# A hybrid attention encoder layer in fp32 on one core: where the exponentials of the first query tiles are kept, and which engine casts and sums them

## The chip, the cores and the metric

The program runs on one core of a Trainium2 chip. The metric is device time in microseconds (us), the median of three runs. One execution was also profiled, instruction by instruction.

The core's engines work side by side, each through its own list of instructions in order: TensorE (PE: matmuls; PEld: its weight loads), VectorE (DVE), ScalarE (ACT), GpSimd (POOL), and SyncE (SP), which issues the DMAs. Matmuls write PSUM, which the kernel uses as eight banks of 128x512 fp32. VectorE and ScalarE read and write PSUM and SBUF; GpSimd's work here is all on SBUF tiles.

## The reference, cut to what matters

One encoder layer over 2048 tokens of width 1024. One input projection feeds two groups of attention heads; the change concerns group A, global attention with 8 query heads on 2 key/value heads of 64 columns.

```python
def global_attention(q, k, v):        # group A; B is windowed, |i - j| <= 128, with a sink logit
    ...
    def one_block(qi):
        s = jnp.einsum('bqkgd,bskd->bkgqs', qi, k).astype(jnp.float32) * scale
        p = jax.nn.softmax(s, axis=-1).astype(v.dtype)
        return jnp.einsum('bkgqs,bskd->bqkgd', p, v)
...
out_a = global_attention(qa, ka, va)
out_b = window_attention(qb, kb, vb, sink_b[l])
mixed = jnp.concatenate([rms_norm(out_a, group_norm_a[l]),
                         rms_norm(out_b, group_norm_b[l])], axis=-1) @ w_out[l]
x = x + rms_norm(mixed, norm_mix_post[l])
h = rms_norm(x, norm_ffn_pre[l])
f = (jax.nn.silu(h @ w_gate[l]) * (h @ w_up[l])) @ w_down[l]
x = x + rms_norm(f, norm_ffn_post[l])
```

## The kernel before

The kernel goes through four stages: input projection with group B's attention (from the start to about 486 us), group A's attention with the output projection (to about 1285 us), the FFN's gate and up products, and its down product. The inner matmuls take fp32r operands, and precision is kept by splitting a value in two: `hi`, the value cast to fp32r, and `lo`, the rest, value minus `hi`; products with `hi` and `lo` are added up in PSUM.

Group A is swept in units (t, g, kt): query tile t (16 tiles of 128 queries), key/value head g (2), key tile kt (16), so 32 units per tile. `attn` writes one unit as:

- two matmuls put the scores, 128 keys by 4 heads x 128 queries, into a PSUM bank (`sc`; the tiles are named `mm`, three banks, and `a`; in tile 0 `ow`, `o` and two `a` as well);
- ScalarE takes the exponential, as a rule in place in that bank; with t < `T_PF` and kt in `DVE_HI0` it goes to an SBUF tile `pfa` instead, of which there are `N_PF` = 2;
- `pha`, the cast to fp32r, by VectorE where kt is in `DVE_HI0` (t < `T_HI`) or `DVE_HI` (later tiles), else by ScalarE;
- `pla` = exponential - `pha`, by VectorE: the bank (or `pfa`) is free after it;
- the softmax's denominator needs the sum of all exponentials over the keys. For kt in `POOL_KT0` (t < `T_PK`) or `POOL_KT` (later) GpSimd adds `pha` to a running tile `acc` (of n such units n-1 adds); for the other kt TensorE does it, with one more matmul of `pha` by a ones matrix (`pha,z`);
- four units later (`AHEAD`), two matmuls of `pha` and `pla` with the values (`vt`).

Behind each (t, g) the sum `acc` is split (`aha`, `ala`) and added by two matmuls, and the denominator goes through DMAs to a reciprocal (`dena`, `cmpa`). The output projection of tile t-1 (`ow<-wo`) is interleaved with tile t from tile 2 on. Tile 0 and the start of tile 1 are interleaved with the tail of group B (its names: `pf`, `ph`, `pl`, `RB`, `R2B`, `VB`, `K1B`, `rb`, `oT`).

Every operation goes through a recorder (so all have line L515 in the profile), and a planner then lists them per engine: it simulates the engines with the cost formulas of `Plan.cost`, picks for each engine the first operation that could start, ranks anew, and keeps the best of four passes. Any edit of `attn` therefore moves other instructions too. `Plan.cost` prices a cast of an SBUF tile at 69 + 0.52 n ns, one of a PSUM bank at 69 + 1.042 n, and a subtraction at 69 + 1.042 n wherever its operands lie.

A second copy of the attention and all behind it, `general`, stands under a condition at the end and isn't executed with these inputs.

Of the kernel before, what the change touches and what calls it, by code (L numbers as in the profile page):

```python
# [10 lines left out]
F32 = mybir.dt.float32  # L11
F32R = mybir.dt.float32r
AF = mybir.ActivationFunctionType
# [5 lines left out]
P = 128  # L19
S = 2048  # L20
D = 1024
NT = S // P
# [17 lines left out]
NM = 5  # L40
LAG = AHEAD + LATE + RC + NM + 2
POOL_KT = tuple(k for k in range(NT) if k != 7)
POOL_KT0 = tuple(k for k in range(NT) if k not in (3, 7, 11))
DVE_HI = (2, 6, 10)
DVE_HI0 = (1, 3, 5, 7, 9, 11, 13)
PREP_NS = 500
P1W = 16000
XP_NS = 400
# [22 lines left out]
WD_L = 13  # L71
WD_R = 3
TAIL = 3
N_PF = 2
T_PF = 3
B_DVE = 13
B_DVE_U = (0, 2)
T_HI = 3
T_PK = 2
DEN_UP = 3000.0  # L80
HALF_UP = 8000.0
LAST_UP = 5000.0
# [5 lines left out]
def f32(ap):  # L88
    return ap.bitcast(F32)
# [428 lines left out]
class Layer:  # L518
# [743 lines left out]
    def attn(self):  # L1262
        nc = self.nc
        units = [(t, g, kt) for t in range(NT) for g in range(2) for kt in range(NT)]
        pend, acc, XY, out, later, norm = {}, {}, {}, {}, {}, {}
        for u in range(len(units) + AHEAD + LATE + 6):
            self.unit = u
            if u < len(units):
                t, g, kt = units[u]
                if g == 0 and kt == 8:  # L1270
                    self.qt.pop(t - 1, None)
                    self.load_q(t + 1)
                if t == g == 0 and kt == 0 and not self.shifted:
                    self.load_kv(NT // 2 - 1)
                if self.shifted and g == kt == 0:
                    self.load_shift(t)
                R1 = self.qt[t]
                sc = self.s_bank(t, g)
                k = self.k_part(self.kt[kt // 2], kt % 2)[:, g * P:(g + 1) * P]
                nc.tensor.matmul(sc, lhsT=k, rhs=R1[:, g, :], start=True, stop=False)  # L1280
                nc.tensor.matmul(sc, lhsT=k, rhs=self.qs[t, g], start=False, stop=not self.shifted)
                if self.shifted:
                    nc.tensor.matmul(sc, lhsT=self.ones_row, rhs=self.sh_row[t][:, g, :], start=False, stop=True)
                pf = sc
                if t < T_PF and kt in DVE_HI0 and not self.shifted:
                    pf = self.kv.tile([P, 512], F32, tag="pfa", bufs=N_PF, name="pfa")
                nc.scalar.activation(pf, sc, AF.Exp, scale=self.up_s if self.shifted else 1.0)
                sc = pf
                ph = self.kv.tile([P, 512], F32R, tag="pha", bufs=NPH, name="pha")
                pl = self.kv.tile([P, 512], F32R, tag="pla", bufs=NPL, name="pla")  # L1290
                if kt in (DVE_HI if t >= T_HI else DVE_HI0):
                    nc.vector.tensor_copy(ph, sc)
                else:
                    nc.scalar.activation(ph, sc, AF.Copy)
                nc.vector.tensor_tensor(pl, sc, f32(ph), op=ALU.subtract)
                if kt in (POOL_KT if t >= T_PK else POOL_KT0):
                    a = acc.get((t, g))
                    if a is None:
                        acc[t, g] = ph
                    elif a.dtype == F32R:  # L1300
                        acc[t, g] = self.kv.tile([P, 512], F32, tag="acc", name="acc")
                        nc.gpsimd.tensor_tensor(acc[t, g], f32(a), f32(ph), op=ALU.add)
                    else:
                        nc.gpsimd.tensor_tensor(a, a, f32(ph), op=ALU.add)
                pend[u] = ph, pl
                yield 432
            if 0 <= u - AHEAD < len(units):
                t, g, kt = units[u - AHEAD]
                ph, pl = pend.pop(u - AHEAD)
                f, l = kt == 0, kt == NT - 1  # L1310
                if f:
                    XY[t, g] = self.xy_banks(t, g)
                X, Y = XY[t, g]
                v = self.v_part(self.vt[kt // 4], kt % 4)[:, g * 192:(g + 1) * 192]
                nc.tensor.matmul(X, lhsT=v[:, 0:P], rhs=ph, start=f, stop=l)
                nc.tensor.matmul(Y, lhsT=v[:, HD:192], rhs=pl, start=f, stop=False)
                if kt not in (POOL_KT if t >= T_PK else POOL_KT0):
                    nc.tensor.matmul(Y, lhsT=self.z1, rhs=ph, start=False, stop=False)
                if l:
                    if g == 0:  # L1320
                        first = t == 0 and not self.shifted
                        pool = self.kv if first else self.op
                        out[t] = (pool.tile([P, 512], F32, tag="oa", bufs=1 if first else 2, name="oa"),
                                  pool.tile([P, 512], F32, tag="dena", bufs=1, name="dena"),
                                  self.sm.tile([16, HD], F32, tag="cmp", bufs=2, name="cmpa"))
                    oa = out[t][0]
                    nc.scalar.activation(oa[ROWS[g]], X[HD:P], AF.Copy)
                    nc.vector.tensor_tensor(oa[ROWS[g]], X[0:HD], oa[ROWS[g]], op=ALU.add)
                    later[u + LATE] = t, g
                yield 432  # L1330
            if u in later:
                t, g = later.pop(u)
                oa, den, cmp = out[t]
                X, Y = XY.pop((t, g))
                a = acc.pop((t, g))
                ah = self.kv.tile([P, 512], F32R, tag="aha", bufs=1, name="aha")
                al = self.kv.tile([P, 512], F32R, tag="ala", bufs=1, name="ala")
                nc.scalar.activation(ah, a, AF.Copy)
                nc.vector.tensor_tensor(al, a, f32(ah), op=ALU.subtract)
                nc.tensor.matmul(Y, lhsT=self.z1, rhs=ah, start=False, stop=False)  # L1340
                nc.tensor.matmul(Y, lhsT=self.z1, rhs=al, start=False, stop=True)
                if t < NT - 1:
                    self.den_row(den, Y, cmp, g)
                else:
                    self.urgent(HALF_UP)
                    nc.scalar.activation(den[ROWS[g]], Y[HD:P], AF.Copy)
                nc.vector.tensor_tensor(oa[ROWS[g]], Y[0:HD], oa[ROWS[g]], op=ALU.add)
                self.urgent(0.0)
                if g == 1:
                    norm[u + (RC if t < NT - 1 else 1)] = t, 0  # L1350
                yield 432
            if u in norm:
                t, j = norm.pop(u)
                oa, den, cmp = out[t]
                if t == NT - 1:
                    self.normalize(oa, den, j)
                    done = j == 3
                    norm[u + 1] = t, j + 1
                elif j == 0:
                    self.recip(cmp, self.RDA[t])  # L1360
                    self.spread(den, self.RDA[t])
                    done = False
                    norm[u + NM] = t, 1
                else:
                    nc.vector.tensor_tensor(oa, oa, den, op=ALU.mult)
                    done = True
                if done:
                    norm.pop(u + 1, None)
                    self.fin[t] = oa
# [444 lines left out]
```

## Time and profile before

| | |
|---|---|
| median of 3 runs | 2609.32 us (2606.59 to 2612.66) |
| the profiled execution | 2609.2 us; its span, first to last instruction, 2607.5 us |
| busy in the span | PE 2485.7 us, DVE 2008.2, POOL 1486.2, ACT 1411.9 |

The profile gives busy times by engine, the busy share in 40 slices of the span (65.2 us each), groups of like instructions, the waits, and the same for any stretch. "Busy" of PE counts the time in which some matmul is under way, at whatever clock; "PEclk" is the granted clock, with 1.00 for 2.4 GHz.

### The profile page before, as it was taken

The page shows a single profiled execution, that of the slowest core. Times are in us where ns is not written, and L with a number is a line of the kernel's source. Part 1 is how long each engine was busy: PE and PEld are TensorE (multiplying, and loading weights), DVE is VectorE, ACT ScalarE, POOL GpSimd, SP SyncE. Part 2 cuts the span into 40 slices and gives each one's busy share as a digit, 9 for nine tenths or more (in the row PEclk, how much of TensorE's full clock was granted, in tenths as well). Part 3 has the DMA queues.
Part 4 walks back from the last instruction along what each step waited for, and adds up shares of the span by engine and source line. Part 5 has one row for each costly group of instructions (what it writes and reads, how often), then busy time and mean ns, then how long its engine had stood idle before and what let it go on. Part 6 is the DMA issues. An engine that isn't in the chain of part 4 may idle for free.

```text
span 2607.5 us, 34089 instructions
## 1 busy us (share of the span) xinstructions
PE 2485.7 (95%) x10636; PEld 1957.9 (75%) x10636; DVE 2008.2 (77%) x3028; ACT 1411.9 (54%) x2622; POOL 1486.2 (57%) x1124
## 2 busy tenths in 40 slices
PE   8999999888999999999999999999999999999997
PEld 6666666555777778777778888778888887888886
DVE  7888887889889998988886767787566566556665
ACT  5666665666888888877543333343323324433443
POOL 3333333458989899999546566655465453422333
PEclk9999999999999999999999999999999999999999
DMA  5233332414222121333354455463332327654564
GB/s 163 100 124 124 123 98 81 142 41 171 68 69 99 56 94 65 114 110 106 106 172 143 146 178 161 155 217 130 108 107 89 113 86 228 191 177 149 182 197 155
DMA packets 187839, 334.88 MB, mean 128 GB/s; under 512 B 23808, under 2 KB 77440, under 8 KB 187136
## 3 DMA queue, kind: packets, MB, share of 16 engines
q1 hardware_dynamic: 187648, 332.61, 38.9%
q8 instruction: 86, 1.41, 0.2%
q14 instruction: 105, 0.86, 0.1%
HBM read 221.46 MB, written 106.56 MB: 126 GB/s over the span
## 4 chain that ended last, share of the span: by engine, by line
PE 57%; DVE 3%; POOL 2%; issue 2%; DMA 1%; ACT 0%; SPq 0%; DVEq 0%; POOLq 0%; ACTq 0%
PE gu L515 29%; PE gv L515 18%; PE ow L515 3%; PE mm L515 3%; PE o L515 3%; PE a L515 2%; POOL acc L515 1%; DVE pla L515 0%; DVE xl L515 0%; DVE wl L515 0%; DVE st L515 0%; POOL C L515 0%; DVE C L515 0%; DVE al L515 0%; DVE c L515 0%
## 5 line engine op out<-in xcount | busy, mean ns | idle before, releaser
L515 POOL TENSOR_TENSOR acc<-acc,pha 128x512 f32<-128x512 f32 x408 | 576.8, 1418 | 71.1 <-ACT pha L515 31.1
L515 POOL TENSOR_TENSOR s<-wraw 128x512 f32<-128x512 f32 x88 | 127.7, 1469 | 319.4 <-DMA wraw<-in_w_up_dram 167.9
L515 PE MATMUL gu<-xh,wl 128*128 128x512 f32 x776 | 279.6, 397 | 5.0 <-DVE wl L515 5.0
L515 PE MATMUL gu<-xh,wh 128*128 128x512 f32 x776 | 281.4, 397 | 0.6 <-ACT wh L515 0.6
L515 PE MATMUL mm<-R,kt 128*128 128x512 f32 x740 | 262.9, 403 | 18.9 <-DVE pla L515 16.5
L515 PE MATMUL gu<-xl,wh 128*128 128x512 f32 x776 | 279.8, 397 | 0.0
L515 PE MATMUL pp<-w_in,xh 128*128 128x512 f32 x720 | 239.8, 406 | 13.7 <-ACT w_in L515 9.2
L515 DVE TENSOR_TENSOR pla<-mm,pha 128x512 fp32r<-128x512 f32 x349 | 231.8, 679 | 22.6 <-ACT pha L515 15.6
L515 ACT ACTIVATE wh<-s 128x512 fp32r<-128x512 f32 x176 | 110.0, 629 | 254.1 <-PE gu L515 136.3
L515 DVE TENSOR_TENSOR al<-ar,ah 128x512 fp32r<-128x512 f32 x154 | 137.8, 900 | 134.7 <-ACT ah L515 115.4
L515 POOL TENSOR_TENSOR c<-c,c 128x512 f32<-128x512 f32 x132 | 200.2, 1531 | 63.9 <-DVE c L515 48.6
L515 ACT ACTIVATE mm<-mm 128x512 f32<-128x512 f32 x349 | 203.3, 590 | 44.6 <-PE mm L515 37.5
L515 ACT ACTIVATE ah<-ar 128x512 fp32r<-128x512 f32 x154 | 96.6, 629 | 206.1 <-PE gu L515 136.6
L515 DVE TENSOR_TENSOR c<-gu,c 128x512 f32<-128x512 f32 x174 | 117.5, 684 | 103.1 <-PE gu L515 98.0
L515 DVE TENSOR_TENSOR wl<-s,wh 128x512 fp32r<-128x512 f32 x176 | 172.6, 987 | 24.4 <-PE gu L515 18.4
L515 PEld LDWEIGHTS mm<-R,kt 128*128 128x128 f32 x740 | 138.1, 191 | 62.2 <-DVE pla L515 30.5
L515 ACT ACTIVATE wh<-wraw 128x512 fp32r<-128x512 f32 x132 | 83.1, 630 | 185.6 <-PE gu L515 92.5
L515 PE MATMUL ow<-wo,oh 128*128 128x512 f32 x488 | 176.6, 396 | 0.6 <-DVE ms L515 0.6
L515 PEld LDWEIGHTS gu<-xh,wl 128*128 128x128 f32 x776 | 146.1, 189 | 40.4 <-DVE wl L515 6.2
L515 PEld LDWEIGHTS gu<-xh,wh 128*128 128x128 f32 x776 | 146.3, 189 | 35.0 <-ACT wh L515 1.1
L515 PEld LDWEIGHTS gu<-xl,wh 128*128 128x128 f32 x776 | 146.6, 189 | 34.3
L515 PEld LDWEIGHTS pp<-w_in,xh 128*128 128x128 f32 x720 | 134.8, 191 | 47.3 <-ACT w_in L515 10.7
(268 smaller groups left out, 6720.9 us busy)
## 6 DMA issues: line engine op xcount, KB each, us to landing
AC<-c SPq DMA_DIRECT2D x154, 256.0 KB
ar<-AC SPq DMA_DIRECT2D x154, 256.0 KB
wdr<-in_w_down_dram SPq DMA_DIRECT2D x99, 256.0 KB
wraw<-in_w_gate_dram SPq DMA_DIRECT2D x20, 1024.0 KB
wraw<-in_w_up_dram SPq DMA_DIRECT2D x20, 1024.0 KB
st<-XB SPq DMA_DIRECT2D x40, 256.0 KB
QA<-RA SPq DMA_DIRECT2D x16, 512.0 KB
R<-QA SPq DMA_DIRECT2D x64, 128.0 KB
```

Source lines behind the costliest of these rows:

```text
L515: op.call(*[real(a) for a in op.args], **{k: real(v) for k, v in op.kw.items()})
```

## The change

In `attn` the exponentials of all units are now taken in place in PSUM; the two `pfa` tiles are gone (`N_PF`, `T_PF`). The tables for the first tiles change:

| per (t, g) of 16 units | before, t = 0 | t = 1 | t = 2 | after, t = 0 | t = 1 | t = 2 | both, t >= 3 |
|---|---|---|---|---|---|---|---|
| exponentials in `pfa` | 7 | 7 | 7 | 0 | 0 | 0 | 0 |
| casts on VectorE | 7 | 7 | 7 | 5 | 3 | 3 | 3 |
| units summed by GpSimd | 13 | 13 | 15 | 11 | 15 | 15 | 15 |
| ones matmuls on TensorE | 3 | 3 | 1 | 5 | 1 | 1 | 1 |

So from t = 1 on every tile is now treated as those from t = 3 on were before.

```diff
--- before.py
+++ after.py
@@ -40,9 +40,9 @@
 NM = 5
 LAG = AHEAD + LATE + RC + NM + 2
 POOL_KT = tuple(k for k in range(NT) if k != 7)
-POOL_KT0 = tuple(k for k in range(NT) if k not in (3, 7, 11))
+POOL_KT0 = tuple(k for k in range(NT) if k not in (2, 5, 8, 11, 14))
 DVE_HI = (2, 6, 10)
-DVE_HI0 = (1, 3, 5, 7, 9, 11, 13)
+DVE_HI0 = (1, 4, 7, 10, 13)
 PREP_NS = 500
 P1W = 16000
 XP_NS = 400
@@ -71,12 +71,10 @@
 WD_L = 13
 WD_R = 3
 TAIL = 3
-N_PF = 2
-T_PF = 3
 B_DVE = 13
 B_DVE_U = (0, 2)
-T_HI = 3
-T_PK = 2
+T_HI = 1
+T_PK = 1
 DEN_UP = 3000.0
 HALF_UP = 8000.0
 LAST_UP = 5000.0
@@ -1281,11 +1279,7 @@
                 nc.tensor.matmul(sc, lhsT=k, rhs=self.qs[t, g], start=False, stop=not self.shifted)
                 if self.shifted:
                     nc.tensor.matmul(sc, lhsT=self.ones_row, rhs=self.sh_row[t][:, g, :], start=False, stop=True)
-                pf = sc
-                if t < T_PF and kt in DVE_HI0 and not self.shifted:
-                    pf = self.kv.tile([P, 512], F32, tag="pfa", bufs=N_PF, name="pfa")
-                nc.scalar.activation(pf, sc, AF.Exp, scale=self.up_s if self.shifted else 1.0)
-                sc = pf
+                nc.scalar.activation(sc, sc, AF.Exp, scale=self.up_s if self.shifted else 1.0)
                 ph = self.kv.tile([P, 512], F32R, tag="pha", bufs=NPH, name="pha")
                 pl = self.kv.tile([P, 512], F32R, tag="pla", bufs=NPL, name="pla")
                 if kt in (DVE_HI if t >= T_HI else DVE_HI0):
```

The planner's lists show what this makes of the engines' order. First VectorE, in the second half of tile 1 (`oa` closes a head of tile 0 or 1, `ala` a sum). Before:

```order
L515 TENSOR_TENSOR pla<-pfa,pha 128x512
L515 TENSOR_TENSOR oa<-o_5956,oa 64x512
L515 TENSOR_TENSOR pla<-mm,pha 128x512
L515 CAST pha<-pfa 128x512 x2
L515 TENSOR_TENSOR pla<-pfa,pha 128x512
L515 TENSOR_TENSOR pla<-mm,pha 128x512
L515 TENSOR_TENSOR pla<-pfa,pha 128x512
L515 TENSOR_TENSOR ala<-acc,aha 128x512
L515 TENSOR_TENSOR pla<-mm,pha 128x512
L515 CAST pha<-pfa 128x512 x2
L515 TENSOR_TENSOR pla<-pfa,pha 128x512
```

and with the change:

```order
L513 TENSOR_TENSOR oa<-o_5962,oa 64x512
L513 TENSOR_TENSOR pla<-a_6140,pha 128x512
L513 TENSOR_TENSOR pla<-mm,pha 128x512 x2
L513 CAST pha<-mm 128x512
L513 TENSOR_TENSOR pla<-mm,pha 128x512
L513 TENSOR_TENSOR ala<-acc,aha 128x512
L513 TENSOR_TENSOR pla<-a_6190,pha 128x512
L513 TENSOR_TENSOR pla<-mm,pha 128x512 x2
L513 CAST pha<-mm 128x512
L513 TENSOR_TENSOR oa<-a_5953,oa 64x512
L513 TENSOR_TENSOR pla<-mm,pha 128x512
```

The casts and subtractions on `pfa` are gone; nearly all that is left between the closing operations is `pla` from a bank, with a cast from a bank here and there.

Next ScalarE, near the end of tile 2 (`sqo`: squares for the output projection's norm). Before:

```order
L515 ACTIVATE pha<-mm 128x512
L515 ACTIVATE pfa<-a_6607 128x512
L515 ACTIVATE sqo<-oa 128x512
L515 ACTIVATE pfa<-mm 128x512
L515 ACTIVATE pha<-mm 128x512
L515 ACTIVATE mm<-mm 128x512 x2
L515 ACTIVATE pfa<-a_6660 128x512
L515 ACTIVATE pha<-mm 128x512
L515 ACTIVATE pfa<-mm 128x512
L515 ACTIVATE aha<-acc 128x512
```

and with the change:

```order
L513 ACTIVATE pha<-mm 128x512
L513 ACTIVATE mm<-mm 128x512 x2
L513 ACTIVATE pha<-mm 128x512
L513 ACTIVATE sqo<-ob 128x512
L513 ACTIVATE a_6624<-a_6624 128x512
L513 ACTIVATE mm<-mm 128x512
L513 ACTIVATE pha<-a_6624 128x512
L513 ACTIVATE mm<-mm 128x512
L513 ACTIVATE pha<-mm 128x512
L513 ACTIVATE mm<-mm 128x512
L513 ACTIVATE pha<-mm 128x512
```

Each exponential is now in place, and ScalarE has a `pha` for 13 of the 16 units of a head, where it had 9.

Last GpSimd, from the end of tile 0 over tile 1 into tile 2; each `acc<-pha` begins the sum of the next (t, g), sometimes ahead of the last adds of the one before. Before:

```order
L515 AFFINE_SELECT pf<-pf 128x512
L515 TENSOR_TENSOR acc<-acc,pha 128x512 x4
L515 TENSOR_TENSOR acc<-pha 128x512
L515 TENSOR_TENSOR acc<-acc,pha 128x512 x10
L515 TENSOR_TENSOR acc<-pha 128x512
L515 TENSOR_TENSOR acc<-acc,pha 128x512 x10
L515 TENSOR_TENSOR acc<-pha 128x512
L515 TENSOR_TENSOR acc<-acc,pha 128x512 x11
L515 TENSOR_TENSOR acc<-pha 128x512
```

and with the change:

```order
L513 AFFINE_SELECT pf<-pf 128x512
L513 TENSOR_TENSOR acc<-acc,pha 128x512 x3
L513 TENSOR_TENSOR acc<-pha 128x512
L513 TENSOR_TENSOR acc<-acc,pha 128x512 x12
L513 TENSOR_TENSOR acc<-pha 128x512
L513 TENSOR_TENSOR acc<-acc,pha 128x512 x10
L513 TENSOR_TENSOR acc<-pha 128x512
L513 TENSOR_TENSOR acc<-acc,pha 128x512 x13
L513 TENSOR_TENSOR rg<-ms,mhalf 128x1
L513 TENSOR_TENSOR acc<-pha 128x512
```

From the first `acc<-pha` shown up to the fourth there were 34 adds and are now 38: tile 1 has 14 adds per head in place of 12. (Tile 0, ahead of these rows, has 10 in place of 12.)

TensorE's list is the same up to tile 0, moves in tiles 0 to 3, and differs in a few dozen places later; SyncE's moves about 20 DMAs by some places, all in tiles 0 to 3 (loads of `vt` and `R`, and group B's small ones).

## Rows read from the trace of the kernel before

**Rows 1.** The page, its head, parts 1 and 2.

```profile
span 2607.5 us, 34089 instructions
PE 2485.7 (95%) x10636; PEld 1957.9 (75%) x10636; DVE 2008.2 (77%) x3028; ACT 1411.9 (54%) x2622; POOL 1486.2 (57%) x1124
...
PE   8999999888999999999999999999999999999997
...
DVE  7888887889889998988886767787566566556665
```

**Rows 2.** Busy by stretch, tiles 0 to 4: us, PE, PEld, DVE, ACT, POOL, PEclk, DMA, GB/s.

```profile
486.00:558.00 72.00, 60.91 (x220) 41.08 (x218) 67.87 (x121) 46.47 (x93) 39.79 (x30) 0.91 0.17 52
558.00:608.00 50.00, 40.47 (x141) 28.30 (x141) 46.18 (x58) 30.99 (x59) 37.04 (x25) 0.90 0.50 194
608.00:657.00 49.00, 39.84 (x152) 27.67 (x150) 48.56 (x61) 33.30 (x62) 39.30 (x27) 0.97 0.20 66
657.00:704.00 47.00, 44.77 (x194) 35.90 (x195) 41.30 (x62) 37.93 (x72) 42.01 (x33) 1.00 0.19 63
704.00:748.00 44.00, 43.21 (x188) 34.49 (x187) 36.75 (x56) 37.09 (x68) 40.47 (x32) 1.00 0.18 60
```

**Rows 3.** Waits, 558.4 to 657.3 us: us in total, times, longest.

```profile
ACT pfa L515 <- DVE pla L515: 10.2, 9, 2.2
PEld mm L515 <- DVE pla L515: 8.8, 11, 2.2
...
PE mm L515 <- DVE pla L515: 4.8, 5, 1.8
```

**Rows 4.** Stretches, `pla` alone (PE, PEld, DVE); then VectorE's work on `pfa`.

```profile
486.00:657.00 171.00, 36.19 (x90) 17.99 (x90) 78.93 (x93) 0.92 0.27 97
...
486.00:558.00 72.00, 23.69 (x27) 0.91 0.17 52
558.00:608.00 50.00, 24.92 (x27) 0.90 0.50 194
608.00:657.00 49.00, 28.93 (x28) 0.97 0.20 66
```

**Rows 5.** Groups, whole span: operation, form, count, busy, mean ns, idle before.

```profile
L515 DVE TENSOR_TENSOR pla<-mm,pha 128x512 fp32r<-128x512 f32 x349 | 231.8, 679 | 22.6 <-ACT pha L515 15.6 <-PE a L515 3.2 <-PE o L515 1.2
L515 DVE CAST pha<-mm 128x512 fp32r<-128x512 f32 x78 | 53.0, 679 | 2.1 <-POOL acc L515 1.5
L515 ACT ACTIVATE pha<-mm 128x512 fp32r<-128x512 f32 x271 | 157.4, 602 | 6.6 <-PE o L515 0.2
```

**Rows 6.** The tile `pfa`: shortest, median and longest in ns.

```profile
L515 DVE CAST pha<-pfa x42: 406/872/1514, 490.1 to 657.4; 128x512 fp32r<-128x512 f32 x42
L515 DVE TENSOR_TENSOR pla<-pfa,pha x42: 672/1162/1781, 494.4 to 659.9; 128x512 fp32r<-128x512 f32 x42
```

**Rows 7.** GpSimd's adds, from 480 to 670 us and from 704.9 to 1066.6 us.

```profile
L515 POOL TENSOR_TENSOR acc<-acc,pha 128x512 f32<-128x512 f32 x71 | 108.7, 1539 | 34.1 <-ACT pha L515 19.3 <-DVE pha L515 6.8 <-ACT mr L515 3.5
...
L515 POOL TENSOR_TENSOR acc<-acc,pha 128x512 f32<-128x512 f32 x206 | 287.4, 1396 | 26.2 <-ACT pha L515 9.2 <-DVE pha L515 5.2
```

**Rows 8.** Timeline in tile 4, two units on bank `a`: start, length.

```profile
715.28 0.63 PE L515 MATMUL a<-R,kt 128*128 128x512 f32 x2
...
717.61 0.69 DVE L515 TENSOR_TENSOR pla<-a,pha 128x512 fp32r<-128x512 f32 x1 [0.47 <-PE a L515]
...
729.62 0.63 PE L515 MATMUL a<-R,kt 128*128 128x512 f32 x2
...
733.51 0.68 DVE L515 TENSOR_TENSOR pla<-a,pha 128x512 fp32r<-128x512 f32 x1
```

**Rows 9.** Two stretches of the FFN, columns as in the second group.

```profile
1400.00:1500.00 100.00, 100.00 (x441) 80.96 (x440) 71.36 (x91) 34.60 (x58) 53.45 (x39) 1.00 0.42 140
...
1800.00:1900.00 100.00, 100.00 (x433) 81.04 (x432) 63.27 (x77) 30.99 (x51) 49.97 (x34) 1.00 0.29 95
```

## The prediction

> **What bounds the kernel now.** The page says TensorE: busy 95% of the span [rows 1]. But that is an average. Of the 40 slices, the early ones and slices 7 to 9 stand at 8 for TensorE; in the latter, about 456 to 652 us, VectorE is at 8 to 9 [rows 1]. That is where group A starts, and there the change is made. So the second view is the busy time by stretch, cut where ScalarE starts the first exponential of a tile: tile 0 from 486 us, then 558, 608, 657, 704 and 748 us. (Three tiles have 96 units; 93 subtractions `pla` stand in the first three stretches, since they lag a little [rows 4].) The reader is to see in [rows 2] that VectorE is busy 67.9 of 72 us in tile 0, 46.2 of 50 in tile 1 and 48.6 of 49 in tile 2, while TensorE is busy only 40.5 and 39.8 us in tiles 1 and 2, partly at a lowered clock (0.90 and 0.97). Tiles 3 and 4, where no new `pfa` is made, have VectorE at 41.3 of 47 and 36.8 of 44 us, TensorE at 95 to 98%, its clock at 1.00, and 36 to 53 more matmuls. Tile 4 does more in 44 us than tile 1 in 50.
>
> The third view, the waits, says the same from the other side: the longest that end in VectorE's work are for `pla`: ScalarE for a free `pfa` 10.2 us, TensorE's loads for a bank 8.8, its matmuls 4.8 [rows 3]. So tiles 0 to 2 are bound by VectorE, about 171 us of the span.
>
> **The change part by part.** *VectorE loses the work on `pfa`*: 23.7, 24.9 and 28.9 us in the three stretches [rows 4]. In its place come 14 `pla` from a bank per tile, and 10, 6 and 6 casts from a bank, all at 0.679 us [rows 5]: 24 x 0.679 = 16.3 us in tile 0, 20 x 0.679 = 13.6 us in tiles 1 and 2 each. Net: -7.4, -11.3 and -15.3 us, 34 us in all.
>
> The gain comes from where the operand lies, and less from the fewer casts. On `pfa` the median cast takes 872 ns and the median subtraction 1162, but the fastest 406 and 672 [rows 6]; from a bank both take 679 on average. The slow ones coincide with GpSimd's adds, which are slow there too, 1539 ns against 1396 later [rows 7]. The Trainium skill (VectorE: DVE Perf Modes, "Why PSUM operands drop a tier") speaks against the change: an fp32 copy within SBUF can run at twice the rate that any PSUM operand allows. The 406 ns copy is that case, the median of 872 is not; the Trainium skill (SBUF — State Buffer, "SBUF: two separate sides") also has a VectorE operation with two SBUF inputs and a GpSimd one lock each other out, and the spread of the subtractions, 672 to 1781 ns, agrees. By the tiers alone the sum would be no change (a rival below), by the means 2590 us. I take the means of this stretch, not the fastest; the other choice is a rival below.
>
> *ScalarE gains casts*: 4, 8 and 8 at 0.602 us [rows 5], so 46.5 + 2.4 = 48.9, 31.0 + 4.8 = 35.8 and 33.3 + 4.8 = 38.1 us. The exponentials cost it the same in place. At tile 4 it has 37.1 us in 44 [rows 2]: covered, if narrowly; were a tile to take less than 38 us, it would be the bound.
>
> *GpSimd*: 4 adds fewer in tile 0, 4 more in tile 1. Tile 1 then has 28 adds, as tile 2 has: 28 x 1.396 = 39.1 us [rows 7], about 40 with the small operations. This is the new floor for tiles 1 and 2; tile 4 has 40.5 [rows 2].
>
> *TensorE*: 4 ones matmuls more in tile 0, 4 fewer in tile 1; at 44 us for 188 matmuls [rows 2], 0.23 us each, 0.9 us each way, beside waits that are longer.
>
> *Banks*: 14 units per tile now hold a bank until `pla` ends. In tile 4 two units on bank `a` hold it 715.28 to 718.30 and 729.62 to 734.19, 3.0 and 4.6 us [rows 8]. With four banks that allows a unit every 0.8 to 1.15 us, and 32 units in 24 to 37 us: not the bound, at that speed of VectorE.
>
> *SyncE and the planner*: DMAs change places in tiles 0 to 3. I cost that at nothing, since the longest waits of this stretch end in work of the engines [rows 3], not in a DMA; a load that came late would delay single units by a microsecond or two. From tile 4 on the orders are nearly the same, and the FFN runs with TensorE at 100% [rows 9], so what is won early stays won.
>
> **The sum.** Tile 0: if VectorE's idle 4.1 us stay, 72 - 7.4 = 64.6 us. Bounds: 72 (group B's chain through its DMAs holds the tile, no gain) and 60.9, where TensorE's own busy time ends it. Tiles 1 and 2: they become what tile 4 is, less its output projection. Bounds: 47 us (tile 3, the worst near row without `pfa`) and 40 (GpSimd). I take 43.5, near tile 4's 44, because GpSimd's list is the same there and TensorE's spare time shortens little once GpSimd is at 90%. Gains: 7.4 + 6.5 + 5.5 = 19.4 us; by the bounds 0 + 3 + 2 = 5 to 11.1 + 10 + 9 = 30. The profiled execution took 2609.2 us, practically the median of the runs, 2609.32: **2609.2 - 19.4 = 2589.8, said as 2590 us**, and by the bounds 2579 to 2604.
>
> **The rivals.**
>
> *Half the gain: tile 0 stays, GpSimd and ScalarE take over at once.* For it: with 36 to 38 us of ScalarE and 40 of GpSimd, each in order, tiles 1 and 2 may go at tile 3's 47 us, and tile 0's pace may come from group B's chain. Against it: tile 4. It gives 2609 - 3 - 2 - 1 = 2603 us.
>
> *The relief isn't there: the long durations move elsewhere.* If GpSimd's collisions are what is conserved, they fall on the other SBUF operations (`ala`, `pl`, `oa`), and the undisturbed prices count: before 42 x (0.406 + 0.672) = 45.3 us, after 22 x 0.679 + 42 x 0.679 = 43.5, a gain of 1.8 us, 2607: no change. For it: the fastest `pfa` operations are that fast [rows 6]. It is what follows from the Trainium skill's tiers (same section) taken alone. Against it: in tile 4 few SBUF operations are left for GpSimd to collide with, and VectorE is at 36.8 us.
>
> *Slower: the banks.* In tiles 0 to 2 `pfa` freed a bank after the exponential. If VectorE's queue stays long (group B's runs of band operations in tile 0), every unit holds a bank for h us. Head 0 of tile 0 has five banks in rotation, head 1 three, partly lent to group B; tiles 1 and 2 have four: 16h/5 + 16h/3 + 2 x 32h/4 = 24.5h us in place of 171. It decides at h = 7.0; at 7.5 us it gives 184, so 2622 us. For it: the waits for banks are there even with `pfa` [rows 3]. Against it: 3.0 and 4.6 us once VectorE has room [rows 8].
>
> **How the numbers follow.** The forecast (2579 to 2604) has a chance of 0.62, half the gain 0.20, no relief 0.09, the banks 0.09. The runs of the kernel before lie within 0.13% of their median, so a change below about 0.2% (5 us) can't be told from none. Faster than 2604: 0.62 and most of the 0.20, so 0.80; within: the no-relief case and a little of the half, 0.11; slower: the banks, 0.09. The range 2577 to 2607 leaves out the banks, some gain past the bounds, and little else.
>
> **What the profile after would show.** No `pfa`; `pla` 0.68 us throughout; VectorE's busy time about 60, 35 and 33 us in tiles 0, 1 and 2, no longer the fullest engine in tiles 1 and 2; GpSimd at 90% or more in these, adds near 1.40 us; tile 0 some 65 us long, tiles 1 and 2 between 42 and 45; the waits of TensorE's loads for `pla` well below 8.8 us; a granted clock nearer 1.00 in tiles 1 and 2; all from tile 4 on as before, only earlier. Wrong would be: tiles 1 and 2 at 47 us or more, TensorE waiting for `pla` longer than before (banks), or tile 0 at 70 us with its waits on group B's DMAs.

## The result, and the profile after

The changed kernel takes 2578.12 us (median of 4 runs, 2575.85 to 2580.17), the kernel before 2608.62 us in the runs beside it (2606.59 to 2612.66). The ratio is 0.9885, with a 95% interval of 0.9872 to 0.9897: 30 us faster, by an interval of 27 to 33. The profiled execution took 2577.71 us.

The page of the changed kernel, head and part 1 (answers to [rows 1]):

```profile
span 2576.0 us, 34105 instructions
PE 2474.4 (96%) x10636; PEld 1951.7 (76%) x10636; DVE 1976.7 (77%) x3008; ACT 1419.9 (55%) x2642; POOL 1472.2 (57%) x1124
```

VectorE lost 31.5 us of busy time and the span lost 31.5 us. That the two are equal is chance: in experiments 1 and 3 below VectorE loses 16.1 and 40.7 us over the whole span, and the span 23.5 and 28.6. Where the time came from is read from the stretches, cut as before at the first exponential of tiles 0 to 4 (us, PE, PEld, DVE, ACT, POOL, PEclk, DMA, GB/s; answers to [rows 2]):

```profile
485.00:549.00 64.00, 57.94 (x220) 39.62 (x220) 58.98 (x117) 48.38 (x97) 30.92 (x29) 0.95 0.17 54
549.00:587.00 38.00, 37.59 (x155) 27.96 (x155) 33.63 (x54) 36.20 (x71) 32.62 (x25) 1.00 0.54 204
587.00:628.00 41.00, 38.03 (x148) 27.39 (x146) 36.85 (x53) 35.44 (x68) 37.94 (x30) 0.96 0.37 129
628.00:672.00 44.00, 43.56 (x190) 34.87 (x190) 38.51 (x58) 38.08 (x71) 41.33 (x33) 1.00 0.21 70
672.00:717.00 45.00, 44.09 (x192) 35.22 (x191) 37.97 (x57) 38.00 (x69) 41.35 (x33) 1.00 0.21 62
```

Tiles 0 to 3 took 72, 50, 49 and 47 us [rows 2] and take 64, 38, 41 and 44: 31 us, practically the whole gain. In tile 0 VectorE is still the fullest engine, 59.0 of 64 us. In tile 1 it is busy 33.6 of 38 us, while TensorE has 37.6 and ScalarE 36.2. The rest, from the FFN's first product (`gu<-xh,wh`) to the end, took 1326 us before and takes 1327 now.

The waits of tiles 1 and 2 (us in total, times, longest; answer to [rows 3]):

```profile
DVE pla L513 <- ACT pha L513: 6.0, 12, 1.5
PEld mm L513 <- DVE pla L513: 5.1, 11, 1.4
```

The waits of TensorE for `pla` shrank (loads 8.8 to 5.1 us, matmuls 4.8 to 1.6), and VectorE now waits for ScalarE's casts. The groups of 485 to 628 us (answers to [rows 5] and [rows 7]):

```profile
L513 POOL TENSOR_TENSOR acc<-acc,pha 128x512 f32<-128x512 f32 x64 | 86.4, 1360 | 21.9 <-ACT pha L513 13.6 <-DVE pha L513 6.0
L513 DVE TENSOR_TENSOR pla<-mm,pha 128x512 fp32r<-128x512 f32 x57 | 37.8, 681 | 3.4 <-ACT pha L513 2.7
...
L513 DVE CAST pha<-mm 128x512 fp32r<-128x512 f32 x17 | 11.6, 680 | 0.9 <-ACT mm L513 0.6 <-PE o L513 0.3
```

From a bank, subtraction and cast take 0.68 us here too, and GpSimd's adds fell from 1539 [rows 7] to 1360 ns.

### The profile page after: what moved, and what is told of

It reads as the page before. It is cut to its first block, busy times and chain, and to the rows that moved or that the text cites. A ratio compares the mean times of both kernels' runs of the same rounds, so it can differ in the third digit from the quotient of the medians.

```text
span 2576.0 us, 34105 instructions
## 1 busy us (share of the span) xinstructions
PE 2474.4 (96%) x10636; PEld 1951.7 (76%) x10636; DVE 1976.7 (77%) x3008; ACT 1419.9 (55%) x2642; POOL 1472.2 (57%) x1124
## 5 line engine op out<-in xcount | busy, mean ns | idle before, releaser
L513 POOL TENSOR_TENSOR acc<-acc,pha 128x512 f32<-128x512 f32 x408 | 563.9, 1387 | 56.7 <-ACT pha L513 23.2
L513 DVE TENSOR_TENSOR pla<-mm,pha 128x512 fp32r<-128x512 f32 x370 | 245.5, 679 | 25.4 <-ACT pha L513 20.1
L513 ACT ACTIVATE mm<-mm 128x512 f32<-128x512 f32 x370 | 215.9, 591 | 35.5 <-PE mm L513 31.7
L513 ACT ACTIVATE ah<-ar 128x512 fp32r<-128x512 f32 x154 | 96.7, 630 | 206.1 <-PE gu L513 139.7
```

What stands on the lines that cost most here:

```text
L513: op.call(*[real(a) for a in op.args], **{k: real(v) for k, v in op.kw.items()})
```

## The experiments

The theory: tiles 0 to 2 were bound by VectorE because its operations on `pfa`, in SBUF, run into GpSimd's adds. Rivals: the new tables alone make the gain; the two `pfa` tiles, for which ScalarE waited, were the limit; an SBUF operand is slow by itself.

**1. PSUM alone.** The kernel before, with its old tables and no `pfa`.

```diff
-T_PF = 3
+T_PF = 0
```

> The kernel before with the exponentials of all units in PSUM and the old tables (7 casts per head on VectorE in tiles 0 to 2, sums as before). Theory (VectorE's price of SBUF operands is what bound tiles 0 to 2): VectorE's 77.5 us on pfa become 42 casts and 42 subtractions from a bank at 0.679 us, 57.0 us, so it loses about 20 us and the kernel about as much: 2589 us, give or take 5; casts and subtractions at 0.68 us in the profile. Rival (the tables alone make the gain, fewer casts on VectorE): no change, 2608. Rival (the wait for one of two pfa tiles, and what hangs on it): the whole gain, 2578.

Measured: 2582.42 us, ratio 0.9895 (0.9879 to 0.991). Tiles 0 to 2:

```profile
484.00:550.00 66.00, 59.59 (x227) 41.30 (x226) 63.54 (x123) 47.49 (x94) 36.70 (x33) 0.94 0.18 60
550.00:591.00 41.00, 38.64 (x148) 26.17 (x147) 38.51 (x60) 32.98 (x62) 31.59 (x25) 1.00 0.52 201
591.00:631.00 40.00, 37.80 (x151) 26.94 (x151) 38.98 (x61) 32.11 (x59) 37.24 (x29) 1.00 0.36 118
```

VectorE goes from 162.6 us in these tiles [rows 2] to 141.0: 21.6 us off, close to the 20 expected. The kernel gained 26, so a little more than VectorE lost, and more than the theory's 2584 to 2594 allow. The tables are not needed for most of the gain. By itself this run does not tell the price of the operations from the shortage of `pfa` tiles. In tiles 0 to 2 the granted clock rose as well, from 0.91, 0.90 and 0.97 [rows 2] to 0.94, 1.00 and 1.00; how much of the gain came by it was not tested. (In tile 0 it doesn't show: there the clock was 1.00 in experiment 6, and the tile took 66 us as here.)

**2. The tables alone.** The changed kernel's casts and sums, but `pfa` for the same units as before (the edit as against the kernel before).

```diff
-POOL_KT0 = tuple(k for k in range(NT) if k not in (3, 7, 11))
+POOL_KT0 = tuple(k for k in range(NT) if k not in (2, 5, 8, 11, 14))
...
-DVE_HI0 = (1, 3, 5, 7, 9, 11, 13)
+DVE_HI0 = (1, 4, 7, 10, 13)
+PF_KT = (1, 3, 5, 7, 9, 11, 13)
...
-T_HI = 3
-T_PK = 2
+T_HI = 1
+T_PK = 1
...
-                if t < T_PF and kt in DVE_HI0 and not self.shifted:
+                if t < T_PF and kt in PF_KT and not self.shifted:
```

> The change's tables, but the exponentials of the same seven units per head of tiles 0 to 2 as before go to pfa. Theory: the 42 subtractions stay at some 1.15 us (48 us), only the casts go, 42 at 0.76 us for 22 at about 0.7: VectorE loses about 16 us, so 2593 us, give or take 5. Rival (tables alone): 2578. Rival (two pfa tiles are the limit): no more than a few us, 2605.

Measured: 2586.37 us, ratio 0.9919 (0.9905 to 0.9932). The tile `pfa` (shortest, median, longest ns):

```profile
L516 DVE TENSOR_TENSOR pla<-pfa,pha x42: 616/1156/1835, 495.2 to 642.9; 128x512 fp32r<-128x512 f32 x42
```

and the stretch of tile 2:

```profile
594.00:643.00 49.00, 40.85 (x151) 27.20 (x151) 46.56 (x58) 37.32 (x70) 45.72 (x31) 0.97 0.27 93
```

The subtractions keep their 1156 ns. Tile 2 stays at 49 us, with VectorE at 46.6 and GpSimd at 45.7, both nearly full. Yet the kernel gained 22 us, more than the theory's 11 to 21, and with `pfa` in two tiles as before: most of the gain doesn't depend on their number. Over the whole span VectorE is busy 1990.6 us, 17.6 less than before. The two halves, 26 and 22, are not additive (the change: 30); each takes work off VectorE, by another means.

**3. GpSimd quiet.** The kernel before with `pfa`, but with TensorE adding up nearly all of tiles 0 to 2.

```diff
-POOL_KT0 = tuple(k for k in range(NT) if k not in (3, 7, 11))
+POOL_KT0 = (0, 1)
...
-T_PK = 2
+T_PK = 3
```

> The kernel before, pfa kept, but in tiles 0 to 2 only 2 of the 16 units of a head are summed by GpSimd (one add per head in place of 12, 12 and 14); TensorE sums the others with 14 ones matmuls per head in place of 3, 3 and 1 (70 more matmuls, 16 us at 0.23 us each, in tiles where it idles 10 us or so apiece). Theory (the slow operations on pfa are collisions with GpSimd's adds): median cast near 0.41 us and median subtraction near 0.68, VectorE 30 us less on pfa, and tiles 1 and 2 near 42 us, so 2590, give or take 6. Rival (an SBUF operand is slow by itself here): cast and subtraction keep 0.87 and 1.16 us, and with TensorE's added work the kernel takes 2608 to 2620.

Measured: 2579.12 us, ratio 0.9885 (0.987 to 0.9901). The tile `pfa`:

```profile
L515 DVE CAST pha<-pfa x42: 399/420/870, 487.1 to 630.2; 128x512 fp32r<-128x512 f32 x42
L515 DVE TENSOR_TENSOR pla<-pfa,pha x42: 616/692/1812, 492.3 to 630.7; 128x512 fp32r<-128x512 f32 x42
```

and the stretches of tiles 0 to 2:

```profile
483.00:553.00 70.00, 64.61 (x247) 44.61 (x247) 59.79 (x128) 50.37 (x99) 11.94 (x13) 0.95 0.17 52
553.00:592.00 39.00, 38.09 (x164) 30.29 (x163) 32.61 (x53) 30.44 (x57) 2.95 (x2) 1.00 0.66 254
592.00:635.00 43.00, 42.93 (x187) 34.65 (x186) 36.60 (x66) 33.63 (x62) 4.19 (x3) 1.00 0.24 75
```

This decides the price. With the same operands in the same place, the median cast falls from 872 to 420 ns and the median subtraction from 1162 to 692 [rows 6]: an SBUF operand is not slow by itself, GpSimd's adds make it so. The trace of the kernel before shows the same split: the 13 casts on `pfa` that no operation of GpSimd overlapped took 412 ns on average, the other 29 took 917; of the subtractions 5 took 681, and 37 took 1210.

The kernel gained 29 us, more than the theory's 2584 to 2596 allow, and as much as the change, without moving one exponential. But it got there otherwise: tile 0, with 27 matmuls more on TensorE (247, and 220 in [rows 2]), still takes 70 us, and since GpSimd's own work is gone too, this run doesn't show that all of the gain came through VectorE.

A quiet SBUF cast is quicker than one from a bank (420 and 680 ns). That goes the way of the tier that the Trainium skill has (VectorE: DVE Perf Modes, "Why PSUM operands drop a tier"), though the ratio here is 1.6 and not 2. The quiet subtraction, 692 ns, agrees with the 691 ns that the same page of the Trainium skill gives for an fp32 `tensor_tensor` of 512 elements ("The TRN2 errata — SBUF-src ops pay a fixed extra latency per instruction").

**4. More casts on VectorE.** The changed kernel; with the next four it asks what bounds tiles 1 and 2 now.

```diff
-T_HI = 1
+T_HI = 3
```

> The changed kernel with 5 casts per head on VectorE in tiles 1 and 2 too, in place of 3: 8 casts go from ScalarE to VectorE. What bounds tile 1 now? Theory A (ScalarE, busy 36.2 of 38 us in tile 1): ScalarE loses 2.4 us per tile, tile 1 some 2 us shorter, kernel 2575 to 2577. Theory B (VectorE is still the one to spare): VectorE gains 2.7 us per tile, 2580 to 2583. Theory C (TensorE and GpSimd share the bound by now): no change, 2578 give or take 2.

Measured: 2576.79 us, ratio 0.9873 (0.9855 to 0.989). Tiles 1 and 2:

```profile
553.00:593.00 40.00, 38.50 (x157) 28.16 (x156) 37.92 (x58) 35.44 (x68) 34.52 (x27) 1.00 0.52 195
593.00:631.00 38.00, 35.97 (x142) 24.79 (x141) 36.22 (x56) 32.30 (x62) 35.70 (x28) 1.00 0.41 136
```

The total fits theories A and C alike. But tile 1, which A had 2 us shorter, took 40 us in place of 38, though ScalarE had less to do; tile 2 took 38 in place of 41, with GpSimd's adds as they were.

**5. No casts on VectorE** in tiles 1 and 2.

```diff
-                if kt in (DVE_HI if t >= T_HI else DVE_HI0):
+                if kt in (DVE_HI if t >= 3 else () if t else DVE_HI0):
```

> The changed kernel with all casts of tiles 1 and 2 on ScalarE: 12 casts go from VectorE to it, 3.6 us per tile. Theory A (ScalarE bounds tile 1): tile 1 at 40 to 41 us in place of 37.5, tile 2 about as long as before or a little longer, kernel 2581 to 2585. Theory B (VectorE): faster by 2 to 4 us. Theory C: no change.

Measured: 2580.52 us, ratio 0.9888 (0.9871 to 0.9904). Tile 1 took 41 us, ScalarE 38.4 of them, as theory A had it; tile 2 took 40. Neither 4 nor 5 can be told from the changed kernel in its total, since the intervals overlap. In the profiles tile 1 is longer with fewer casts on ScalarE as well as with more, so that ScalarE bounds it is not shown.

**6. Fewer adds on GpSimd** in tiles 1 and 2.

```diff
+POOL_KT1 = tuple(k for k in range(NT) if k not in (3, 7, 11))
...
-                if kt in (POOL_KT if t >= T_PK else POOL_KT0):
+                if kt in (POOL_KT if t >= 3 else POOL_KT1 if t >= T_PK else POOL_KT0):
...
-                if kt not in (POOL_KT if t >= T_PK else POOL_KT0):
+                if kt not in (POOL_KT if t >= 3 else POOL_KT1 if t >= T_PK else POOL_KT0):
```

> The changed kernel with 13 of 16 units per head summed by GpSimd in tiles 1 and 2, in place of 15: 4 adds fewer per tile (5.5 us of GpSimd), 4 ones matmuls more (0.9 us of TensorE). If GpSimd, 39.3 of 41.5 us, bounds tile 2 (the floor of the prediction): tile 2 at 38 to 39 us, kernel 2574 to 2576. If it can lag and catch up: tile 1 unchanged or 1 us longer, tile 2 at 41 to 42, kernel 2578 to 2580.

Measured: 2575.51 us, ratio 0.987 (0.9853 to 0.9886). Tiles 1 and 2:

```profile
550.00:587.00 37.00, 36.81 (x151) 26.94 (x150) 32.08 (x51) 35.05 (x68) 31.22 (x24) 1.00 0.57 218
587.00:626.00 39.00, 36.84 (x155) 27.80 (x154) 36.14 (x55) 35.98 (x70) 35.26 (x28) 1.00 0.35 124
```

Tile 2 shortens from 41 to 39 us, as it should if GpSimd held it up there, but in experiment 4 it shortened more with all its adds. The total agrees (2 to 4 us less were expected, 2.6 came), but it is not clear of the change's interval. That GpSimd bounds tile 2 is not shown.

**7. Three banks** in tiles 1 and 2.

```diff
-        return self.bank(self.ps_a, "a1") if self.ns % 4 == 0 else self.mm_bank()
+        return self.bank(self.ps_a, "a1") if t > 2 and self.ns % 4 == 0 else self.mm_bank()
```

> The changed kernel with three score banks in tiles 1 and 2 in place of four (bank a is left out). By the prediction's rule for banks, 32 units x hold / banks, with the hold of 4.3 us that the order of scores and subtractions gives after the change: 46 us per tile in place of 37.5 and 41.5, so 2590. If banks are far from the bound: no change, 2578. If the engines' queues let the hold shrink with the banks (3.0 us is the shortest seen): 32 us, hidden, and 2578 to 2583.

Measured: 2578.99 us, ratio 0.9887 (0.9871 to 0.9904): no change. Tile 1 took 41 us and tile 2 42, not 46. A bank less costs tile 1 some 3 us in this profile, and the rule that multiplies units by a fixed hold fails: the hold is partly waiting, and shrinks. On the banks named `mm`, from the start of an exponential to the end of its subtraction, it took 3.0 us in tile 1 and 3.7 in tile 2 with the change, and takes 2.6 and 2.9 here.

**8. Casts and adds together** (4 and 6).

```diff
+POOL_KT1 = tuple(k for k in range(NT) if k not in (3, 7, 11))
...
-T_HI = 1
+T_HI = 3
...
-                if kt in (POOL_KT if t >= T_PK else POOL_KT0):
+                if kt in (POOL_KT if t >= 3 else POOL_KT1 if t >= T_PK else POOL_KT0):
...
-                if kt not in (POOL_KT if t >= T_PK else POOL_KT0):
+                if kt not in (POOL_KT if t >= 3 else POOL_KT1 if t >= T_PK else POOL_KT0):
```

> The changed kernel with 5 casts per head on VectorE and 13 of 16 units summed by GpSimd in tiles 1 and 2 (the two single edits together). If both engines hold these tiles up in turn: tiles 1 and 2 together at 73 to 75 us in place of 79 (75 with the fewer adds alone), kernel 2573 to 2575. If TensorE is the bound once the adds are fewer: as with the fewer adds alone, 2575 to 2576.

Measured: 2577.48 us, ratio 0.9877 (0.9862 to 0.9892). Tiles 1 and 2 took 38 us each, 76 together, not less than with 6 alone. No version here beats the changed kernel by more than the measurement can tell.

Two things weaken what 4 to 8 say of single tiles. From the first exponential of tile 0 to that of tile 4 the changed kernel took 186.9 us, and 4, 6 and 8 took 187.2, 187.1 and 187.4 (5 took 191.5, and 7 took 188.6): what tiles 1 and 2 win, tiles 0 and 3 pay. And the rest of the kernel from the FFN's first product on, which these edits don't concern, took between 1321 and 1331 us in the profiles of experiments 4 to 8, which is more than their totals differ by (5 us). So what bounds tiles 1 and 2 now stays open.

**9. The opposite, elsewhere.** The changed kernel with `pfa` in tiles 3 to 15.

```diff
-                nc.scalar.activation(sc, sc, AF.Exp, scale=self.up_s if self.shifted else 1.0)
+                pf = sc
+                if t >= 3 and kt in (1, 3, 5, 7, 9, 11, 13) and not self.shifted:
+                    pf = self.kv.tile([P, 512], F32, tag="pfa", bufs=2, name="pfa")
+                nc.scalar.activation(pf, sc, AF.Exp, scale=self.up_s if self.shifted else 1.0)
+                sc = pf
```

> The changed kernel with the opposite done where nothing was changed: in tiles 3 to 15 the exponentials of kt 1, 3, 5, 7, 9, 11 and 13 go to two pfa tiles, with casts and sums as they are. Theory (price of SBUF operands beside GpSimd): 14 subtractions per tile at about 1.15 us in place of 0.68, VectorE +6.6 us per tile, from 37 to 45 us to 44 to 51; GpSimd's adds 0.1 us slower, +3 us per tile. Tiles of 44 to 47 us become 47 to 51: 13 tiles x 3 to 4 us, kernel 2615 to 2630. Rival (TensorE bounds these tiles, and a faster release of banks helps or does nothing): 2570 to 2580.

Measured: 2658.77 us, ratio 1.0196 (1.0182 to 1.0209), 81 us above the changed kernel. Part 1 of its page, and the stretches of tiles 4 and 5:

```profile
PE 2501.2 (94%) x10636; PEld 1954.4 (74%) x10636; DVE 2073.4 (78%) x3008; ACT 1427.6 (54%) x2642; POOL 1535.4 (58%) x1124
...
676.00:725.00 49.00, 45.45 (x192) 34.62 (x190) 46.10 (x57) 37.58 (x70) 46.48 (x33) 1.00 0.18 57
725.00:779.00 54.00, 47.63 (x195) 37.15 (x194) 51.58 (x65) 39.70 (x72) 45.15 (x33) 0.94 0.22 76
```

and two groups of 760 to 1150 us:

```profile
L513 POOL TENSOR_TENSOR acc<-acc,pha 128x512 f32<-128x512 f32 x193 | 299.8, 1554 | 36.3 <-ACT pha L513 13.4 <-DVE pha L513 11.8 <-DVE ms L513 1.3
L513 DVE TENSOR_TENSOR pla<-pfa,pha 128x512 fp32r<-128x512 f32 x105 | 118.2, 1126 | 10.0 <-ACT pha L513 7.2 <-PE mm L513 1.5 <-PE o L513 0.6
```

The sign was right, the size too small: 2615 to 2630 was expected. VectorE's busy time grew by 96.7 us (2073.4, and 1976.7 with the change), most of it in the 182 subtractions of 13 tiles, the rest in its other operations on SBUF tiles. GpSimd's grew by 63.2 us; between 720 and 1080 us of the changed kernel its adds took 1411 ns, here 1554. So the idle time of VectorE, which is busy 329 of 360 us in that stretch of the changed kernel, took up some 16 us, far less than the forecast had let it. TensorE's loads for the banks `mm` waited 65.9 us for `pla` from tile 3 on, and 17.9 in the changed kernel; ScalarE waited 16.0 us for a free `pfa`. What the number of `pfa` tiles cost by itself was not tested.

## Why the prediction was right, and where it was off

- **The number:** 2590 us forecast, 2578.1 measured. That is inside the stated range (2577 to 2607), but by 1 us, and past the 2579 that the sum's own bounds reach. The direction and the mechanism were right; that the number lies in the range at all owes something to luck.
- **That VectorE bounds tiles 0 to 2, and that its work on `pfa` is what to count:** right. The forecast was 7.4, 11.3 and 15.3 us off VectorE in tiles 0, 1 and 2, and 8.9, 12.6 and 11.7 came: 33 us, and 34 forecast. Experiments 1 to 3 take work off VectorE by three means and gain 22 to 29 us, 9 puts `pfa` where it was not, and loses 81. Each of the three gained more than its theory gave, so VectorE's time is not the whole account; the rise of the granted clock in tiles 0 and 1 is a rival for the rest.
- **Means, not the fastest rows:** right. The rival of no relief rested on the fastest operations; experiment 3 shows that these are the ones that GpSimd leaves alone, and after the change the collisions did not simply move elsewhere: GpSimd's adds fell to 1360 ns.
- **Tile 0, 64.6 us:** 64, with VectorE still the fullest (59.0 us, forecast about 60).
- **Tiles 1 and 2 at 43.5 us: the step that was mis-sized.** They took 38 and 41. The failing sentence is that GpSimd's 28 adds of 39.1 us, about 40 with the small operations, are "the new floor for tiles 1 and 2". The adds were priced at 1396 ns and took 1360, so 28 of them make 38.1 us. And a tile was cut at its exponentials, but GpSimd need not have added them up by then: in tile 1's 38 us it did 25 adds of its 28, so it was some 5 adds behind by the end of the tile (2 of them from tile 0) and handed them on; in tile 2's 41 us it did 29. It was busy 86% of tile 1 and 93% of tile 2, where 90% or more was forecast for both. In tile 1 TensorE (37.6 of 38 us) and ScalarE (36.2), which the prediction had as the bound of a tile under 38 us, are the fullest. Which engine sets the pace of tiles 1 and 2, experiments 4 to 8 don't settle.
- **Tile 3, taken as unchanged:** 47 to 44 us. It had taken over a backlog: 4 matmuls more fell into it (194 against 190). So its 47 us were a poor lower bound for a tile without `pfa`. That the backlog is the cause was read from the profiles, not tested.
- **The sum:** 19.4 us forecast, 31.5 in the spans. The missing 12 are 5.5 in tile 1, 2.5 in tile 2, 3 in tile 3 and about 1 in tile 0 and the rounding of the cuts.
- **Half the gain** did not come: with 36.2 us of ScalarE tile 1 still took 38. **The banks** did not bind: three do nearly as well as four (7).
- **The granted clock** went to 1.00 in tile 1, as forecast, but fell from 0.97 to 0.96 in tile 2, where it was to come nearer 1.00; in tile 0 it rose from 0.91 to 0.95.
- **A misreading without effect:** of the early slices only the first, not several, stands at 8 for TensorE [rows 1].

## What to carry to other kernels

Price an operation by the mean in its own stretch, and ask which engine makes it long: here an fp32 operation of VectorE from SBUF to SBUF had 1.7 to 2.1 times its quiet median beside GpSimd's adds, and lengthened these; an operand in PSUM, or a quiet GpSimd, took both away. A floor worked out from one engine's work per tile holds only for an engine that cannot hand work on to the next tile; look for its slack before using it. Take a bound from a stretch that owes nothing to the one before it. And before a tile's length is put down to one engine, look at the tiles around it: what one wins another may pay.

## What was not expected of the hardware

The collision is mutual and strong: the cast's median 420 ns quiet and 872 beside the adds, the subtraction's 692 and 1162, the adds' mean 1539 beside `pfa` and 1360 without it in the first tiles, 1554 and 1411 in the later ones. In experiment 9 the kernel grew by 81 us for 97 us more of VectorE's busy time, though VectorE and GpSimd had both been idle 8 to 9% of that stage (busy 329 and 331 of 360 us between 720 and 1080 us of the changed kernel).
